# A LoRA-adapted linear layer: TensorE and ScalarE in loops with waits on register counts, VectorE without drains, no early store

## The chip, the cores and the metric

The kernel runs on one core of a Trainium2 chip. The metric is the device time of one execution in microseconds (us); the span, a little shorter, is the time from the first to the last instruction in the profile. "PE" is TensorE, "PEld" its weight loads, "DVE" is VectorE, "ACT" is ScalarE, "POOL" is GpSimd, "SP" is SyncE, the engine that issues the large transfers; a "q" behind a name (PEq, SPq) is the engine's sequencer. The DMA engines, of which the page counts sixteen for this core, move data between the chip's memory (HBM) and the core's on-chip memory (SBUF). A semaphore is a counter that one engine raises and another waits for. A "drain" is the instruction that the kernel before puts behind some of VectorE's copies, and that then raises the semaphore for which a store waits; DRAIN in the trace. A "table load" is the ACT_TABLE_LOAD record that the trace shows on ScalarE. The "granted clock" is TensorE's clock as the profile gives it, 1.00 being full speed (PEclk in the slices, in tenths).

A program on one core has no second die to compare with; a run counts as slow only when it is over 1.5% above the fastest of its kernel.

## The reference

```python
# x: (16, 2048, 256), W: (256, 256), A: (256, 16), B: (16, 256), E: (16,), scale = 1.0, all float32
x_flat = x.reshape(-1, 256)                  # 32768 rows
y = x_flat @ W
lora_out = ((x_flat @ A) * E) @ B
return (y + scale * lora_out).reshape(16, 2048, 256)
```

The kernel folds the second term into the weights once: `weff = W + A diag(E) B scale`. After that it is one product of 32768 rows with a 256 x 256 matrix. 33.5 MB of x must be read and 33.5 MB of y written.

## The kernel before

The rows are cut into 8 chunks of 4 MB. A chunk lies in one of 6 SBUF buffers ("homes"), and the result is written back into the home that its input came from. A chunk is worked on in 8 groups of 4 x 128 rows. Each group passes through four engines:

1. POOL casts it to bf16 (`stage`).
2. PE transposes it into PSUM, the memory that PE's results go to in this kernel ("turn").
3. ScalarE copies the transposed group to SBUF (`xt`).
4. PE multiplies it with `weff` and VectorE copies the result home.

The parts that the change touches, with cuts marked:

```python
ORDER = ["L0", "L1", "L2", "L3", "L4", "L5",            # L: load a chunk, S: store a chunk
         "S0", "S1", "L6", "L7", "S2", "S3", "S4", "S5", "S6", "S7"]
EARLY_AFTER = 1
NS, NX, NT, NY = 2, 4, 4, 2      # buffers of stage, xt, psum_xt, psum_y
UNROLL = 4
# ... (SyncE: all large transfers, in one queue)
        for step in ORDER:
            c = int(step[1:])
            if step[0] == "L":
                # ... load chunk c; L5 waits for weff, L6 and L7 wait until S0 and S1 have landed
                if c == EARLY_AFTER:
                    sync.wait_ge(s_first, 1)             # first group of the result is home
                    sync.dma_start(out=y_chunks[0, :16, 0, :32], in_=home(0)[:16, 0, :32]).then_inc(s_early, 16)
            else:
                sync.wait_ge(s_chunk, c + 1)
                # ... (S0 also waits for the early store)
                sync.dma_start(out=y_chunks[c], in_=home(c)[:]).then_inc(...)
# ... (ScalarE)
        for g in range(N_GROUPS):                        # 64, written out
            scalar.wait_ge(s_turned, g + 1)
            if g >= NX:
                scalar.wait_ge(s_y, g - NX + 1)
            scalar.copy(out=xt[g % NX][:], in_=halves).then_inc(s_xt, 1)
# ... (VectorE)
        for g in range(N_GROUPS):
            vector.wait_ge(s_y, g + 1)
            vector.tensor_copy(out=home(c)[:, b:b + CG, :], in_=psum_y[g % NY][:]).then_inc(s_free, 1)
            if g == 0:
                vector.drain().then_inc(s_first, 1)
            if g % GPC == GPC - 1:
                vector.drain().then_inc(s_chunk, 1)
# ... (PE)
        def take(s):
            tensor.wait_ge(s, 1).then_inc(s, -1)         # wait for the semaphore, then take it down
        # turn(i): take(s_stage), then 4 transposes; multiply(i): take(s_xt), take(s_free), then 8 matmuls
        with tensor.Fori(0, N_GROUPS // UNROLL):
            for i in range(UNROLL):
                turn(i + 2)
                multiply(i)
```

POOL holds back chunk 5 until stores S0 and S1 have landed; the change leaves that as it is.

## Time and profile before

| | before |
|---|---|
| time, median of the first 3 runs | 161.84 us (161.71 to 161.97) |
| span of the profiled run | 160.5 us |
| bytes of the large transfers | 67.11 MB |
| a 32 KB packet on one DMA engine | 1213 to 1220 ns almost everywhere |
| pace of a group | 1.31 us |
| last result copied home | 122.0 us |

The page cuts the span into 40 slices of 4 us. A digit is the busy share in tenths; "GB/s" is what the DMA engines moved. Four rows of it:

```profile
PE   0585979999999999400019999999990000000000
...
PEclk9999999999999999955555999999998555555555
DMA  7999999999999999999999999999999999999993
GB/s 262 432 425 466 449 393 425 490 392 408 498 400 392 492 400 400 400 417 466 425 400 451 457 392 433 474 402 425 466 400 433 466 408 433 449 425 417 441 449 155
```

The DMA row is full from the second slice to the last but one. PE stops after 30 of the 40 slices and pauses in the middle. The page's line for the queue that carries x and y (packets, MB, share of the 16 engines' span), and its account of the chain of work that ended last:

```profile
q1 hardware_dynamic: 2624, 67.11, 97.9%
...
PE 11%; DVE 1%; issue 0%
```

The chain covers 12% of the span and, listed in order of time, ends at 122 us with a VectorE copy. After that there are 38 us of nothing but stores. The page's groups of instructions (line, engine, operation, tiles, count; then busy us and the mean ns of one; then the engine's idle time before them and what ended most of it; the lines of the weight loads are left out):

```profile
L213 DVE COPY home<-psum_y 128x1024 f32<-128x1024 f32 x64 | 78.3, 1225 | 30.0 <-PE psum_y L236 25.3
L173 POOL CAST stage<-home 128x1024 bf16<-128x1024 f32 x64 | 66.3, 1040 | 47.5 <-PE psum_xt L228 21.4
L193 ACT COPY xt<-psum_xt 128x1024 bf16<-128x1024 bf16 x64 | 64.7, 1012 | 49.8 <-PE psum_xt L228 49.8
L236 PE MATMUL psum_y<-weff,xt 128*128 128x256 bf16 x512 | 69.4, 281 | 2.6 <-PEq L221 2.5
L228 PE MATMUL psum_xt<-ident,stage 128*128 128x128 f32 x264 | 42.5, 287 | 18.6 <-PEq L221 18.6
...
L193 ACT ACT_TABLE_LOAD x1 | 1.3, 1283 | 2.5 <-issue 2.5
```

In a steady stretch PE needs 0.44 us for a group's transposes and 0.87 us for its matmuls, without a gap: 1.31 us, more than any other engine needs for a group. So PE sets the pace of compute. The SyncE queue in order of time (start us, us from first to last issue, what):

```profile
0.00 2.44 SPq L131 DMA_DIRECT2D home<-in_x_dram  x4
16.99 0.36 SPq L144 DMA_DIRECT2D out_dram<-home  x1
17.40 1.84 SPq L131 DMA_DIRECT2D home<-in_x_dram  x4
28.16 10.82 SPq L149 DMA_DIRECT2D out_dram<-home  x2
72.43 10.03 SPq L131 DMA_DIRECT2D home<-in_x_dram  x2
82.51 39.88 SPq L149 DMA_DIRECT2D out_dram<-home  x6
```

The line at 16.99 us is the early store. The first two large stores are issued at 28 and 39 us, but in the record of single packets their first bytes move at 61 and 71 us: loads L2 to L5 stand ahead of them in the queue. The last store is issued at 122 us and moves at 148 us. And the longest waits of that queue (us in total, times, longest):

```profile
SPq L149 <- DVEq L217: 52.9, 6, 10.4
SPq L131 <- DMA out_dram<-home: 42.8, 2, 33.4
...
SPq L144 <- DVEq L215: 14.5, 1, 14.5
```

### The profile page before, as it was taken

What the parts mean: (1) busy time and instruction counts of PE and PEld (TensorE: products, weight loads), DVE (VectorE), ACT (ScalarE), POOL (GpSimd) and SP (SyncE); (2) the same over time, 40 slices, a digit from 0 to 9 for tenths busy, and PEclk for the clock granted to TensorE, in tenths of its full rate; (3) what the DMA queues carried; (4) which work ended last, traced back from release to release, by engine and by line L of the source; (5) the groups of instructions that cost most, each with busy time, mean ns of one, the idle gap of its engine ahead of it and who ended that gap; (6) DMA issues with size and microseconds to landing.
All of it is one profiled execution on the core that took longest, in us unless ns stands there. A gap on an engine that the chain in (4) does not pass through costs nothing. (4 is left out here: it accounts for less than half of the span.)

```text
span 160.5 us, 2160 instructions
## 1 busy us (share of the span) xinstructions
PE 94.2 (59%) x782; PEld 83.9 (52%) x782; DVE 79.5 (50%) x66; ACT 66.0 (41%) x65; POOL 67.0 (42%) x70
## 2 busy tenths in 40 slices
PE   0585979999999999400019999999990000000000
PEld 0354869999999999300017999899990000000000
DVE  0102796999999999700003799899993000000000
ACT  3240667777777777400005577777740000000000
POOL 1542648777777777000045577777700000000000
PEclk9999999999999999955555999999998555555555
DMA  7999999999999999999999999999999999999993
GB/s 262 432 425 466 449 393 425 490 392 408 498 400 392 492 400 400 400 417 466 425 400 451 457 392 433 474 402 425 466 400 433 466 408 433 449 425 417 441 449 155
DMA packets 2979, 67.43 MB, mean 420 GB/s; under 512 B 528, under 2 KB 544, under 8 KB 672
## 3 DMA queue, kind: packets, MB, share of 16 engines
q1 hardware_dynamic: 2624, 67.11, 97.9%
q10 hardware_dynamic: 352, 0.30, 0.5%
q14 instruction: 3, 0.02, 0.0%
HBM read 33.85 MB, written 33.56 MB: 420 GB/s over the span
## 5 line engine op out<-in xcount | busy, mean ns | idle before, releaser
L213 DVE COPY home<-psum_y 128x1024 f32<-128x1024 f32 x64 | 78.3, 1225 | 30.0 <-PE psum_y L236 25.3
L173 POOL CAST stage<-home 128x1024 bf16<-128x1024 f32 x64 | 66.3, 1040 | 47.5 <-PE psum_xt L228 21.4
L193 ACT COPY xt<-psum_xt 128x1024 bf16<-128x1024 bf16 x64 | 64.7, 1012 | 49.8 <-PE psum_xt L228 49.8
L236 PE MATMUL psum_y<-weff,xt 128*128 128x256 bf16 x512 | 69.4, 281 | 2.6 <-PEq L221 2.5
L236 PEld LDWEIGHTS psum_y<-weff,xt 128*128 128x128 bf16 x512 | 51.4, 101 | 9.6 <-issue 3.2
L228 PE MATMUL psum_xt<-ident,stage 128*128 128x128 f32 x264 | 42.5, 287 | 18.6 <-PEq L221 18.6
L228 PEld LDWEIGHTS psum_xt<-ident,stage 128*128 128x128 f32 x264 | 33.1, 149 | 21.1 <-issue 20.2
L198 DVE TENSOR_SCALAR home<-psum_y,e_sb 16x256 f32<-16x256 f32 x1 | 0.5, 472 | 6.6 <-DMA e_sb<-in_lora_E_dram 6.6
L208 DVE TENSOR_TENSOR weff<-home,psum_y 128x512 bf16<-128x512 f32 x1 | 0.7, 689 | 5.9 <-DMA home<-in_W_dram 5.9
L248 PE MATMUL psum_y<-ident,home 128*16 128x128 f32 x2 | 0.6, 394 | 5.1 <-DMA home<-in_lora_A_dram 5.1
L248 PEld LDWEIGHTS psum_y<-ident,home 128*16 128x16 f32 x2 | 0.1, 87 | 5.1 <-issue 5.1
L193 ACT ACT_TABLE_LOAD x1 | 1.3, 1283 | 2.5 <-issue 2.5
L254 PE MATMUL psum_y<-home 16*128 16x256 f32 x4 | 2.1, 670 | 0.2 <-DMA home<-in_lora_B_dram 0.2
L254 PEld LDWEIGHTS psum_y<-home 16*128 16x128 f32 x4 | 1.2, 319 | 0.8 <-DMA home<-in_lora_B_dram 0.6
L152 POOL MEMSET ident<- 128x128 f32 x1 | 0.2, 204 | 0.7 <-SPq L268 0.7
L154 POOL TENSOR_SCALAR_AFFINE_SELECT ident<-ident 128x128 f32<-128x128 f32 x1 | 0.3, 292 | 0.2 <-POOL ident L152 0.2
L290 POOL MEMSET const-float32-0.0<- 128x1 f32 x1 | 0.1, 98 | 0.2 <-issue 0.2
L290 POOL MEMSET const-bfloat16-1.0<- 128x1 bf16 x1 | 0.1, 101 | 0.0
L290 POOL MEMSET const-uint8-127<- 128x1 uint8 x1 | 0.1, 101 | 0.0
L290 POOL MEMSET const-float32-1.0<- 128x1 f32 x1 | 0.1, 98 | 0.0
## 6 DMA issues: line engine op xcount, KB each, us to landing
out_dram<-home SPq DMA_DIRECT2D x8, 4096.0 KB, 39.7
home<-in_x_dram SPq DMA_DIRECT2D x7, 4096.0 KB, 20.8
home<-in_x_dram SPq DMA_DIRECT2D x2, 1024.0 KB, 5.7
home<-in_x_dram SPq DMA_DIRECT2D x1, 2048.0 KB, 11.5
home<-in_W_dram ACTq DMA_DIRECT2D x1, 256.0 KB, 10.9
home<-in_lora_A_dram ACTq DMA_DIRECT2D x1, 16.0 KB, 4.9
e_sb<-in_lora_E_dram ACTq DMA_DIRECT2D x1, 0.1 KB, 5.5
home<-in_lora_B_dram ACTq DMA_DIRECT2D x1, 16.0 KB, 5.8
```

Of the source, the lines that this page charges most:

```text
L152: gpsimd.memset(ident[:], 0.0).then_inc(s_ident, 1)
L154: gpsimd.affine_select(out=ident[:], in_=ident[:], compare_op=ALU.not_equal, fill=1.0, base=0, pattern=[[-1, P]], channel_multiplier=1,).t ...
L173: gpsimd.tensor_copy(out=stage[g % NS][:], in_=home(c)[:, b:b + CG, :]).then_inc(s_stage, 1)
L193: scalar.copy(out=xt[g % NX][:], in_=halves).then_inc(s_xt, 1)
L198: vector.tensor_scalar(out=ate, in0=psum_y[0][:R, :KT, :P], scalar1=e_sb[:], scalar2=float(scale), op0=ALU.mult, op1=ALU.mult,).then_inc(s ...
L208: vector.tensor_add(out=weff[:], in0=w_sb, in1=psum_y[1][:, :KT, :]).then_inc(s_free, NY)
L213: vector.tensor_copy(out=home(c)[:, b:b + CG, :], in_=psum_y[g % NY][:]).then_inc(s_free, 1)
L228: ins = tensor.transpose(psum_xt[i % NT][:, b, :], words[:, b, :], ident[:])
L236: ins = tensor.matmul(psum_y[i % NY][:, b, :], xt[i % NX][:, b, t, :], weff[:, t, :], start=(t == 0), stop=(t == KT - 1),)
L248: ins = tensor.transpose(psum_y[0][:R, t, :P], a_sb[:, t, :], ident[:])
L254: ins = tensor.matmul(psum_y[1][:, t, :], ate[:, t, :], b_sb, start=True, stop=True)
L290: nc = _bacc.Bacc("TRN2", target_bir_lowering=False, num_devices=1)
```

## The change

Its intent is to take instructions out of the engines' sequencers. PE no longer takes semaphores down; in its loop it waits until they have reached a count that it computes in a register. ScalarE's 64 copies become a loop of 8 turns and lose their second wait, which the order on PE now implies. VectorE's copies release the stores themselves, without a drain. The early store goes, and with it SyncE's wait for the first group.

```diff
-EARLY_AFTER = 1
+COPY_UNROLL = 8
+LEAD = 2
 # SyncE
-                if c == EARLY_AFTER:
-                    sync.wait_ge(s_first, 1)
-                    sync.dma_start(out=y_chunks[0, :16, 0, :32], in_=home(0)[:16, 0, :32]).then_inc(s_early, 16)
             else:
-                sync.wait_ge(s_chunk, c + 1)
-                if c == 0:
-                    sync.wait_ge(s_early, 16)
+                sync.wait_ge(s_free, NY + GPC * (c + 1))
 # ScalarE
-        for g in range(N_GROUPS):
-            scalar.wait_ge(s_turned, g + 1)
-            if g >= NX:
-                scalar.wait_ge(s_y, g - NX + 1)
-            # ... copy
+        with scalar.Fori(0, N_GROUPS, COPY_UNROLL) as g0:
+            for g in range(COPY_UNROLL):
+                scalar.wait_ge(s_turned, g0 + (g + 1))
+                # ... copy
 # VectorE
-            if g == 0:
-                vector.drain().then_inc(s_first, 1)
-            if g % GPC == GPC - 1:
-                vector.drain().then_inc(s_chunk, 1)
 # PE
-        def take(s):
-            tensor.wait_ge(s, 1).then_inc(s, -1)
-        def turn(i):
-            take(s_stage)
+        def turn(i, count, free=None):
+            tensor.wait_ge(s_stage, count)
+            if free is None:
+                tensor.sem_inc(s_stage, -1)
             for b in range(CG):
+                if b == CG - 1 and free is not None:
+                    tensor.wait_ge(s_free, free)
                 # ... transpose
-        def multiply(i):
-            take(s_xt)
-            take(s_free)
+        def multiply(i, count):
+            tensor.wait_ge(s_xt, count)
             # ... 8 matmuls
-        with tensor.Fori(0, N_GROUPS // UNROLL):
+        with tensor.Fori(0, N_GROUPS, UNROLL) as i0:
             for i in range(UNROLL):
-                turn(i + 2)
-                multiply(i)
+                count = i0 + (i + 1)
+                turn(i + LEAD, count, free=count)
+                multiply(i, count)
 # ... (cut: unused semaphores, the two turns ahead of the loop)
```

More of the change, by code (lines that the diff above doesn't have):

```diff
@@ L95 @@
     s_free = sem("y_free")
-    s_chunk = sem("chunk_done")
-    s_first = sem("first_done")
-    s_early = sem("early_stored")
     def home(c):
@@ L187, in scalar_program @@
                 opening.append(ins.ins.name)
-        for g in range(N_GROUPS):
-            scalar.wait_ge(s_turned, g + 1)
-            if g >= NX:
-                scalar.wait_ge(s_y, g - NX + 1)
-            halves = psum_xt[g % NT][:].bitcast(BF16).rearrange("q b (p t) -> q b t p", t=KT)
-            scalar.copy(out=xt[g % NX][:], in_=halves).then_inc(s_xt, 1)
+        assert N_GROUPS % COPY_UNROLL == 0
+        with scalar.Fori(0, N_GROUPS, COPY_UNROLL) as g0:
+            for g in range(COPY_UNROLL):
+                scalar.wait_ge(s_turned, g0 + (g + 1))
+                halves = psum_xt[g % NT][:].bitcast(BF16).rearrange("q b (p t) -> q b t p", t=KT)
+                scalar.copy(out=xt[g % NX][:], in_=halves).then_inc(s_xt, 1)
     def vector_program():
@@ L249, in tensor_program @@
         ins.then_inc(s_pe_set_up, 1)
-        turn(0)
+        turn(0, 1)
         tensor.wait_ge(set_up_loaded["b"], 16)
@@ L255, in tensor_program @@
         ins.then_inc(s_pe_set_up, 1)
-        turn(1)
+        turn(1, 1)
         assert N_GROUPS % UNROLL == 0 and all(UNROLL % n == 0 for n in (NS, NX, NT, NY))
-        with tensor.Fori(0, N_GROUPS // UNROLL):
+        with tensor.Fori(0, N_GROUPS, UNROLL) as i0:
             for i in range(UNROLL):
-                turn(i + 2)
-                multiply(i)
+                count = i0 + (i + 1)
+                turn(i + LEAD, count, free=count)
+                multiply(i, count)
     def wait_for_stores(nc):
```

## The prediction

> **What bounds it now.** The DMA engines. The page's slices show them 0.9 or more busy in 38 of 40 slices; one queue carries 67.1 MB, 97.9% of the 16 engines' span. Single packets in the trace: a 32 KB packet takes 1213 to 1220 ns almost everywhere, 27 GB/s an engine, 432 GB/s for sixteen.[...] 67.1 MB at 432 GB/s is 155.4 of the 160.5 us span. The rest: 1.0 us before the first packet, 0.5 us of slower packets in the first 8 us, 0.5 us per engine where the first store follows the last early load (58 to 61 us, packets of 1.5 to 1.8 us), an uneven finish (engines end between 158.1 and 160.0 us) and 0.5 us of closing.
>
> The chain of waits ends in PE and VectorE work at 122 us, 12% of the span; after it come 38 us of nothing but stores. So that chain isn't the bound.
>
> **Compute and its slack.** A steady group takes 1.31 us on PE (0.44 us for 4 transposes, 0.87 for 8 matmuls), without a gap: PE sets the compute pace (VectorE 1.23, POOL 1.04, ScalarE 1.01). The last chunk is finished at 122 us; its store's first packet moves at 148 us. First store: issued at 28 us, moves at 61 us. Second: 39 against 71 us. POOL idles 18.6 us by design until two stores landed. Some 25 us of slack everywhere.
>
> **What the change removes, adds, moves** (durations from the trace):
> - PE: 194 takes of 51 ns, 9.9 us of sequencer time, mostly hidden behind a full array; added are register additions (36 ns); a compare-and-branch was there already (200 ns here[...]). Steady pace stays 1.31 us.
> - ScalarE: 60 second waits of 17 ns go; 8 loop turns come, estimate 0.2 us a turn, against 0.3 us idle per copy. No effect on PE.
> - VectorE: 9 drains. They last 1.26 us in the trace but begin when the copy does: their own cost is some 30 ns each. Off the path.
> - Early store: 16 packets of 128 bytes, 13 ns each: nothing. The queue engine no longer waits 14.5 us for the first group, so loads 2 to 4 are issued at about 3 to 4 us instead of 17.4 us. But load 1 keeps the DMA engines fed to 22 us: none starved before, gain 0.
> - The last transpose of a group now waits for y being freed: same condition, 0.1 us earlier; at first it delays a turn until the weights are made, about 2 us, in slack.
>
> **On the critical path:** below 0.1 us of about 10 us of removed instruction time. One open term: if the early store had taken a first-write cost off the first large store, the 58 to 61 us stretch grows by up to 1 us.
>
> **Time:** 161.7 us, 8 in 10 between 161.0 and 162.6. Faster by over 2% 0.02, within 2% 0.95, slower 0.03.
>
> **Shows it right:** DMA slices still full; 32 KB packets at 1213 ns; last compute at 118 to 123 us; steady group 1.31 us; SyncE's wait for the first group gone, its waits for stores as long as before.
> **Would make it wrong:** a gap in the DMA slices near 58 to 64 us or 72 to 83 us; loops slowing compute by 20 us in total; slower packets because five loads are queued at once.

The sum behind 161.7 us is 155.4 us of packets and the parts named after it. The 432 GB/s are 16 times 32768 bytes in 1213 ns. The first-write cost of up to 1 us is a supposition, which the run without the early store tests below. In the trace before, the loop that PE has already ends each turn with a compare-and-branch of 200 ns (mean of 16, 76 to 223 ns).

## The result

The changed kernel took 161.78 us (median of 4 runs, 161.60 to 162.15), beside 161.78 us for the kernel before on the same chip (4 runs, 161.56 to 161.97). The ratio is 1.0004, with a 95% interval of 0.9981 to 1.0026: the same. A ratio here and below is the mean time of one kernel's fast runs over that of the other's fast runs of the same rounds, so it is not quite the ratio of the medians that are quoted. Three rows of the slices after:

```profile
PE   0575998999999999600009999999980000000000
...
DMA  7999999999999999999999999999999999999994
GB/s 253 397 433 429 499 400 409 474 425 400 466 441 392 433 433 417 417 400 474 433 392 452 460 392 449 425 433 425 433 441 417 441 450 409 441 449 409 433 458 180
```

The DMA row is as full as before, for as long. The queue's line has 32 packet records fewer, the early store's, and the same bytes. The chain that ended last now reads quite differently, although the two kernels do the same thing in the same time:

```profile
q1 hardware_dynamic: 2592, 67.11, 97.9%
...
DMA 40%; PE 31%; DVE 2%; POOL 1%; SPq 1%; issue 0%; POOLq 0%
```

That account follows semaphores back from the last instruction, and how far it gets depends on how the waits are written. It is no measure of what binds. The groups after, again without the weight loads:

```profile
L204 DVE COPY home<-psum_y 128x1024 f32<-128x1024 f32 x64 | 78.4, 1225 | 28.7 <-PE psum_y L223 23.5
L164 POOL CAST stage<-home 128x1024 bf16<-128x1024 f32 x64 | 66.3, 1040 | 46.3 <-PE psum_xt L216 20.3
L184 ACT COPY xt<-psum_xt 128x1024 bf16<-128x1024 bf16 x64 | 63.8, 1014 | 40.2 <-PE psum_xt L216 39.8
L223 PE MATMUL psum_y<-weff,xt 128*128 128x256 bf16 x512 | 69.0, 280 | 0.0
L216 PE MATMUL psum_xt<-ident,stage 128*128 128x128 f32 x264 | 42.4, 286 | 20.9 <-POOL stage L164 18.0
...
L184 ACT ACT_TABLE_LOAD x8 | 10.3, 1283 | 2.8 <-issue 2.6
```

One line is new in kind: eight table loads on ScalarE where there had been one, one for each turn of its loop. VectorE's copies start 1.31 us apart, as before (median 1310 ns in both traces). The last copy ends at 120.7 us instead of 122.0, mainly because the first two steps after the pause took 2.56 and 1.46 us before and 1.37 and 1.31 us after. That is not a gain of the change. From 84 to 88 us the granted clock was 0.50 in the trace before and 0.67 in the one after. Three later runs are the changed kernel up to its last copy (the ones with a tail, below): two had 0.50 there, a first step of 2.36 and 2.38 us, and a last copy that ended at 122.0 and 121.9 us; the third had 0.66, 1.40 and 120.8 us. SyncE's queue, in order of time, and then its longest waits:

```profile
0.00 14.02 SPq L128 DMA_DIRECT2D home<-in_x_dram  x8
28.95 10.82 SPq L140 DMA_DIRECT2D out_dram<-home  x2
72.89 10.01 SPq L128 DMA_DIRECT2D home<-in_x_dram  x2
82.95 38.16 SPq L140 DMA_DIRECT2D out_dram<-home  x6
```

```profile
SPq L140 <- DVE home L204: 60.9, 6, 14.9
SPq L128 <- DMA out_dram<-home: 42.4, 2, 33.1
...
SPq L128 <- DVEq L200: 9.7, 1, 9.7
```

The early store and its wait of 14.5 us are gone. The wait for stores to land, the one tied to the DMA engines, stays: 42.8 us before, 42.4 us after.

### The profile page after: what moved, and what is told of

It reads as the page before. It is cut to its first block, busy times and chain, and to the rows that moved or that the text cites. A ratio compares the mean times of both kernels' runs of the same rounds, so it can differ in the third digit from the quotient of the medians.

```text
span 160.4 us, 2049 instructions
## 1 busy us (share of the span) xinstructions
PE 93.2 (58%) x782; PEld 83.3 (52%) x782; DVE 79.5 (50%) x66; ACT 74.1 (46%) x72; POOL 67.0 (42%) x70
## 4 chain that ended last, share of the span: by engine, by line
DMA 40%; PE 31%; DVE 2%; POOL 1%; SPq 1%; issue 0%; POOLq 0%
DMA out_dram<-home 27%; PE psum_y L223 20%; DMA home<-in_x_dram 14%; PE psum_xt L216 10%; DVE home L204 2%; POOL stage L164 1%; SPq L128 0%; POOLq L163 0%; SPq L292 0%; POOLq L161 0%; SPq L256 0%
## 5 line engine op out<-in xcount | busy, mean ns | idle before, releaser
L204 DVE COPY home<-psum_y 128x1024 f32<-128x1024 f32 x64 | 78.4, 1225 | 28.7 <-PE psum_y L223 23.5
L184 ACT COPY xt<-psum_xt 128x1024 bf16<-128x1024 bf16 x64 | 63.8, 1014 | 40.2 <-PE psum_xt L216 39.8
L216 PE MATMUL psum_xt<-ident,stage 128*128 128x128 f32 x264 | 42.4, 286 | 20.9 <-POOL stage L164 18.0
L216 PEld LDWEIGHTS psum_xt<-ident,stage 128*128 128x128 f32 x264 | 32.7, 148 | 23.9 <-POOL stage L164 18.6
L184 ACT ACT_TABLE_LOAD x8 | 10.3, 1283 | 2.8 <-issue 2.6
```

The source lines that it names most:

```text
L216: ins = tensor.transpose(psum_xt[i % NT][:, b, :], words[:, b, :], ident[:])
```

## The experiments

Theory 1: the DMA engines are the bound, compute has some 25 us of slack at the last store, and no part of the change is worth anything in this kernel. Rival 1: the parts have real gains and losses that happen to cancel. Rival 2: compute did become cheaper and the DMA only hides it. Eleven kernels were run.

### One part at a time

The first four ran on one chip; the kernel before took 161.84 us there (7 runs, 161.46 to 161.96).

**No early store, and nothing else.**

```diff
 # on the kernel before
-                if c == EARLY_AFTER:
-                    sync.wait_ge(s_first, 1)
-                    sync.dma_start(... early store ...)
-                if c == 0:
-                    sync.wait_ge(s_early, 16)
-            if g == 0:
-                vector.drain().then_inc(s_first, 1)
```

> The kernel before, with only the early store (and the drain that releases it) taken out. Theory (DMA engines bound, the parts are worth nothing here): 161.8 us within 0.4, loads 2 to 4 issued by 5 us instead of 17.4, the packets at 58 to 61 us slow by the same 0.4 to 0.6 us per engine as before. Rival (the change's parts have real gains and losses that cancel): losing the early store costs 0.5 to 1 us, seen as a longer slow stretch where the first large store starts.

Measured: 162.00 us (161.80 to 162.15), ratio 1.0011, interval 0.9992 to 1.0029: the same. The first large store costs no more without the early one. Between 58 and 61 us, packets took longer than 1213 ns by 0.36 us per DMA engine in sum; it was 0.65 us in the kernel before and 0.50 us in the changed one. The open term of the prediction falls. (The stretch varies from trace to trace: 0.59 to 0.72 us in the kernels with the early store, 0.15 to 0.50 us in those without it whose stores are whole.)

**ScalarE's loop, and nothing else.**

```diff
 # on the kernel before
-        for g in range(N_GROUPS):  ...  wait s_turned, wait s_y, copy
+        with scalar.Fori(0, N_GROUPS, COPY_UNROLL) as g0:  ...  wait s_turned, copy
```

> The kernel before, with only ScalarE's program put into a loop of 8 turns. Theory: 161.8 us within 0.4; eight table loads of 1.28 us on ScalarE instead of one, and VectorE's copies still start every 1.31 us, since ScalarE works ahead. Rival (cancelling parts): the seven added table loads, 9 us, delay PE by some of that and cost 0.5 us or more.

Measured: 161.77 us (161.59 to 161.90), ratio 0.9995, interval 0.9978 to 1.0012: the same, with eight table loads and VectorE's median step at 1310 ns. How ScalarE hides a load shows best in the timeline of the changed kernel (start us, us, what, idle time before it):

```profile
45.16 1.01 ACT L184 COPY xt<-psum_xt 128x1024 bf16<-128x1024 bf16 x1 [0.30 <-PE psum_xt L216]
46.19 1.28 ACT L184 ACT_TABLE_LOAD   x1
47.48 3.93 ACT L184 COPY xt<-psum_xt 128x1024 bf16<-128x1024 bf16 x4
51.71 1.01 ACT L184 COPY xt<-psum_xt 128x1024 bf16<-128x1024 bf16 x1 [0.30 <-PE psum_xt L216]
```

Before the load, ScalarE idles 0.30 us ahead of each copy. After it, four copies follow without idling, and then the rhythm is back. PE works two groups ahead with its transposes, so the 1.28 us never reach it: from 16 us on, the trace of the changed kernel has two pauses of PE over 30 ns, at 23.7 us, where POOL waits for load L1, and at 67.0 us, POOL's hold. None is at a table load.

**Drains put back, eight times as many.**

```diff
 # on the changed kernel
             vector.tensor_copy(...).then_inc(s_free, 1)
+            vector.drain().then_inc(s_drained, 1)
 # SyncE
-                sync.wait_ge(s_free, NY + GPC * (c + 1))
+                sync.wait_ge(s_drained, GPC * (c + 1))
```

> The changed kernel, with the drains put back and made eight times as many: one after each of the 64 copies, and stores released by them. Theory: 161.8 us within 0.4; VectorE copies still start every 1.31 us and the last store is issued within 0.1 us of where it is in the changed kernel. Rival (cancelling parts): if eight drains had cost anything, 64 cost eight times that: 0.5 us or more.

Measured: 161.66 us (161.58 to 161.93), ratio 0.9990, interval 0.9974 to 1.0007: the same. But the rest of the expectation was a miss. VectorE's median step became 1361 ns, not 1310: a drain in every group adds 51 ns to the cycle, enough to make VectorE and not PE the pace maker. The last copy ended at 122.8 us, later than in any run of the changed kernel (120.7 to 122.0), where 0.1 us had been allowed for its store. Over 64 groups that is 3.3 us of compute time, and it vanished in the slack. In the kernel before, the one drain per chunk shows as a step of 1.36 us followed by one of 1.26 us: lost and caught up. As VectorE can do a step without a drain in 1.26 us, a drain costs VectorE itself about 0.1 us.

**PE's loop, and nothing else.**

```diff
 # on the kernel before: turn, multiply and the loop as in the change; s_chunk, drains, ScalarE, SyncE as before
```

> The kernel before, with only PE's program as in the changed kernel (waits on counts in registers, no takes). Theory: 161.8 us within 0.4, group pace 1.31 us as before, because the array is full and the 51 ns takes were hidden. Rival (cancelling parts): gains 0.5 us or more that the other parts give back.

Measured: 161.61 us (161.44 to 162.00), ratio 0.9991, interval 0.9968 to 1.0014: the same, median step 1310 ns. In these runs no part moved the time by more than the intervals allow, about 0.3% or 0.5 us either way. So rival 1 has nothing of that size to cancel; smaller parts would not have been resolved.

### How much slack there is

The next four ran on another chip; the kernel before took 161.77 us there (7 runs, 161.55 to 161.80). The changed kernel as it is did not run there, nor on the third chip below; the kernel before stands in for it, since the two took the same time.

**A group's transposes done twice.**

```diff
 # on the changed kernel, in turn, inside the loop only
+            for b in range(CG):
+                tensor.transpose(psum_xt[i % NT][:, b, :], words[:, b, :], ident[:])
```

> The changed kernel, with each group's four transposes done twice (same result): PE needs 1.75 us a group instead of 1.31, 28 us more PE time in all. Theory (DMA engines bound, about 25 us of slack at the last store): 161.8 us within 0.5, last compute at about 128 us instead of 121. If compute sets the time: some 10 us longer or more.

Measured: 162.91 us (162.75 to 163.02), ratio 1.0074, interval 1.0057 to 1.0091. A group took 1.747 us, and the last copy ended at 130.6 us, still 18 us before its store's turn. So the queue did not wait, and yet the time rose by 1.1 us, where 0.5 had been allowed. Theory 1 was incomplete; the last three runs below look for the rest.

**A group's transposes and matmuls done twice.**

```diff
 # on the kernel of the last run, in multiply
-            for b in range(CG):
+            for b in [*range(CG), *range(CG)]:
```

> The changed kernel, with each group's transposes and matmuls done twice (same result): 2.62 us a group. The slack argument with its due times gives a number here: chunk c is done at about 13.7 + 20.9 (c + 1) + 1.5 us, store 4 (due at 119) is just late, stores 5, 6 and 7 wait for compute, and the end is at the last chunk (183 us) plus one store (about 12 us): 192 to 199 us. If DMA were the bound whatever compute does: 162. If compute already set the time: 84 us of added PE work, 240 us or more.

Measured: 195.75 us (2 runs, 195.36 and 196.14), in the middle of what the due times gave. Its PE and DMA slices (4.87 us each):

```profile
PE   0889999999999999999999999999999999999400
...
DMA  8999999999999999999999997980079205950297
```

PE is now full and the DMA row has holes after the 24th slice: each of the last stores waits for its chunk. The slack argument thus has the right size, not only the right sign.

**Stores cut to an eighth, on both kernels.**

```diff
-                sync.dma_start(out=y_chunks[c], in_=home(c)[:])...
+                sync.dma_start(out=y_chunks[c, :, :4, :], in_=home(c)[:, :4, :])...
```

The output is wrong: 28 of every 32 rows are never written. With so little to store, compute ends last.

> The kernel before, with each store cut to 4 of 32 rows (wrong output on purpose), so that compute and not DMA ends last: expected 105 to 109 us, VectorE copies every 1.31 us.

> The changed kernel with the same small stores. Theory A (PE's array is full at 1.31 us a group, the removed 9.9 us of takes were hidden behind it, the added table loads are hidden too): the same as the cut kernel before within 0.5 us. Theory B (the change does make compute cheaper, the DMA only hides it): 2 to 10 us faster than the cut kernel before. Theory C (the table loads hurt): 1 us or more slower.

Measured: 107.27 us (107.12 to 108.84, the highest one counted as slow) for the kernel before so cut, and 107.91 us (107.26 to 108.04) for the changed one. Their ratios to the uncut kernel before are 0.6630 (0.6616 to 0.6643) and 0.6659 (0.6638 to 0.6680), so the changed one is 1.0044 times the other, with intervals that just overlap. Theory B, rival 2, falls: where compute ends last, the change still gains nothing. The medians lie 0.64 us apart, a little more than the 0.5 us of theory A and less than the 1 us of theory C. The median step is 1310 ns in both. In the two traces the difference goes with waiting for loads: from 16 us on the changed one has three pauses of PE over 30 ns (2.47, 0.56 and 0.61 us), each a wait for a POOL cast just after load L1, L6 or L7 had landed. The other has 1.68 and 0.40 us at L1 and L6 and none at L7, which landed there 0.9 us earlier. The table loads between 30 and 70 us leave no pause. POOL's waits for the loads of x, first the cut kernel before, then the cut changed one (us in total, times, longest):

```profile
POOL stage L173 <- DMA home<-in_x_dram: 12.9, 6, 3.0
```

```profile
POOL stage L164 <- DMA home<-in_x_dram: 15.4, 7, 3.8
```

The change issues loads L2 to L4 at once instead of 14 us later. In the ten traces taken by then, the last semaphore of load L1 came at 22.8 to 23.6 us where the early store and its wait were there (4 kernels) and at 23.7 to 23.9 us where they were not (6 kernels). So loads that are queued early may slow the start by a few tenths of a microsecond. The times don't resolve it (the run without the early store: 1.0011, interval 0.9992 to 1.0029), and no run separated the wait from the store. It stays open.

### Where the 1.1 us came from

In the trace with doubled transposes, one DMA engine has 32 KB packets of mostly 1273 to 1293 ns instead of 1213. The records do not name the engine; that it is one is read from each packet starting where the last one ended, within 13 ns. They occur from 61 to 82 us and from 103 to 132 us: where compute runs beside stores. Where compute runs beside loads (12 to 58 us) there are none of this kind. The kernel before and the changed one have them too, but fewer, since in them POOL's hold stops compute for most of the first stretch. That engine's packets add up, and the span ends with the slowest engine: in this run it finished at 161.0 us, the others by 159.8 us.

To find what slows it, work of one kind was put where the changed kernel computes nothing, after 121 us beside the last stores. The three ran on a third chip; the kernel before took 161.87 us there (7 runs, 161.72 to 162.83).

```diff
 # on the changed kernel; first run: 320 narrow matmuls (40 x 8)
+        tensor.wait_ge(s_free, NY + N_GROUPS)
+        with tensor.Fori(0, 40, 1):
+            for i in range(8):
+                tensor.matmul(psum_y[i % NY][:, 0, :P], xt[0][:, 0, 0, :], weff[:, 0, :P], start=True, stop=True)
 # second run: 128 wide ones (16 x 8), psum_y[i % NY][:, 0:KT, :] and weff[:]
 # third run, instead of PE: 22 copies on VectorE, 26 on ScalarE, 26 on POOL, into spare buffers
```

> Why did turning twice cost 1.1 us when the slack was not used up? In its trace one DMA engine has 32 KB packets some 70 ns longer (1273 to 1293 ns) exactly where compute runs beside stores. Here the changed kernel, with 320 useless 128-column matmuls on PE alone after the last group, beside stores 5 to 7, where nothing computes otherwise. Theory P (PE's work beside stores slows that engine): about 0.07 us per packet of 1.28 us, so 20 us of tail give 16 slow packets and 1.1 us: 162.6 to 163.4 us. Theory Q (it takes the other engines' memory traffic, or all together): 161.8 within 0.4, no slow packets after 122 us.

> The same tail with 128 matmuls of 512 columns: about as long, far fewer instructions. If the slowing goes with PE's being busy: as many slow packets per us, at about 70 ns, as with the narrow tail. If it goes with the number of instructions PE runs[...]: slow packets with a clearly smaller excess, 15 to 30 ns, and a time nearer to 161.8. Under theory Q: 161.8 within 0.4 and none.

> The changed kernel with a tail on VectorE (22 copies out of PSUM), ScalarE (26) and POOL (26) together, PE idle. Theory P: 161.8 us within 0.4, no slow packets after 122 us. Theory Q in the form 'memory traffic of the other engines': slow packets after 122 us and 162.6 us or more.

Measured: 163.42 us (163.21 to 163.99), ratio 1.0096, interval 1.0053 to 1.0139, with the narrow tail; 162.26 us (162.06 to 162.59), ratio 1.0020, interval 0.9981 to 1.0060, with the wide one; 162.26 us (162.15 to 162.62), ratio 1.0020, interval 0.9980 to 1.0059, with the other engines' tail. What the engines did in one stretch of the three tails (window in us, its length, then busy us and instructions of PE, PEld, DVE, ACT and POOL, granted clock, DMA share, GB/s), narrow, wide, others:

```profile
122.00:131.00 9.00, 9.00 (x165) 9.00 (x163) 0.00 (x0) 0.00 (x0) 0.00 (x0) 1.00 1.01 433
```

```profile
122.00:131.00 9.00, 8.91 (x42) 4.10 (x43) 0.00 (x0) 0.00 (x0) 0.00 (x0) 1.00 1.00 433
```

```profile
122.00:131.00 9.00, 0.00 (x0) 0.00 (x0) 8.76 (x8) 8.75 (x9) 8.49 (x9) 0.55 1.01 437
```

PE is busy all the time in the first two, but runs nearly four times as many instructions in the first. The lengthening follows the instructions and not the busy time of PE. The table counts every instruction record of the trace, those of the sequencers too; "lengthened" means longer than 1213 ns by over 5 ns:

| stretch beside stores | records per us | lengthened packets | median excess of these |
|---|---|---|---|
| changed kernel, compute, 103 to 120 us | 21.4 | 13 | 71 ns |
| narrow PE tail, 122 to 138 us | 40.4 | 12 | 127 ns |
| wide PE tail, 122 to 148 us | 11.0 | 20 | 28 ns |
| other engines' tail, 122 to 148 us | 2.8 | 14 | 14 ns |
| changed kernel, nothing running, 122 to 148 us | 0.3 | 1 | 75 ns (the last of the compute stretch) |

For the three stretches with PE that is 2.1 to 2.6 ns for each record of the trace while the packet lasted (71 ns over 21.4 x 1.284 us, 127 over 40.4 x 1.340, 28 over 11.0 x 1.241). The other engines' tail does not fit that figure: 14 ns over 2.8 x 1.227 us are 4.1 ns a record. Of the expectations, theory P had the narrow tail's time about right (163.42 us, 162.6 to 163.4 expected) with half of its excess (70 ns, 127 measured), and it was wrong on the other engines' tail, where it allowed no slow packets. Theory Q was wrong on both PE tails, and the 162.6 us that it gave the other engines' tail was not reached. The 15 to 30 ns expected of the wide tail, if instructions count, were met with 28. So "PE's work" is too coarse: in PE's tails the number of instructions counts, and other engines lengthen packets too; that one rule covers all engines is not shown. The 1.1 us of doubled transposes fit: compute ran beside S0 and S1 as well, and about 20 more packets of one engine were lengthened by some 70 ns.

Two rivals can be checked in the same traces. The narrow tail also keeps PE's weight loads busier, 16.0 of 16 us against 15.1 of 17 us in the changed kernel's compute, which is too little for 127 against 71 ns. And instruction fetches do not fit: the page counts only 2 packets in the queue that it labels "instruction", in the narrow tail's trace at 86.6 and 90.4 us, before the tail begins.

What it is about an instruction that lengthens the packets, no run shows. Every run here was also recorded, with its core's span and clock, so none shows the time without a record. In the kernel before and in the changed one the effect is the same: 21 packets longer by 50 to 100 ns in each, 1.6 us in sum.

## Why the prediction was right

- **The bound.** "The DMA engines", with a full row, 1213 ns for a 32 KB packet, and so 432 GB/s for sixteen engines: unchanged after (median packet 1213 ns in both traces). The run with doubled groups shows the boundary from the other side. When compute took 2.62 us a group, the DMA row got holes and the time became 195.75 us.
- **The slack.** "Some 25 us of slack everywhere" held at the last store. Moving the last copy from 120.7 to 130.6 us left no gap in the queue, and the time from the due dates, 192 to 199 us, was met for the doubled groups. That last copy was still 18 us ahead of its store; the 1.1 us that this run took longer go with the slowed DMA engine, not with the slack.
- **PE.** "Steady pace stays 1.31 us": yes, in the changed kernel, with PE's loop alone, and with the small stores, where compute ends last. The 9.9 us of takes were hidden behind a full array.
- **ScalarE.** Here one term was mis-sized. "8 loop turns come, estimate 0.2 us a turn": a turn costs a table load of 1.28 us (1283 ns for each of the eight; where a copy was ready, it began 11 ns after the load had ended) plus 45 ns for its branch and about 35 ns for each register operation. The conclusion, no effect on PE, held, because ScalarE idles 0.30 us ahead of each copy and works ahead of the multiplication.
- **VectorE.** "Some 30 ns each" was low: about 0.1 us of VectorE's time (a step of 1361 ns with a drain, 1.26 us without). A drain's record lasts 1258 ns, only 33 ns longer than a copy's 1225, and begins 13 to 15 ns after the copy does in the trace before; the cost shows in the steps. Off the path, as said.
- **The early store.** Its packets were worth "nothing", and the open term, a first-write cost of up to 1 us, was not there: 0.36 us of lengthened packets at the first large store without it, 0.65 us with it.
- **The time.** 161.7 us was predicted and 161.78 us measured, inside the range of 161.0 to 162.6 us. The DMA sum behind it carries this; the two mis-sized terms above could not reach the time.

What the prediction didn't have is the one DMA engine that slows with the instructions run beside stores. It listed "an uneven finish" but took it as given. It made no difference here, because both kernels run almost the same instructions in those stretches.

## What to carry to other kernels

Before costing what a change removes, find the resource that is full until the end, and write down when each result is due to it: here a dozen numbers from the queue's timeline gave the slack, and a kernel slowed on purpose confirmed it to within a few us. Ten microseconds taken out of a sequencer were worth nothing here, with the array behind it full and the transfers the bound. When putting ScalarE's work in a loop, look for a table load in each turn (8 loads in 8 turns here, 1 in the form written out): it was hidden here by 0.30 us of idle time per copy. What it costs on a ScalarE that sets the pace, no run shows.
